# Modulation held in row blocks of two tiles, c kept on chip, and a reordered end of the convolution, in a decoder layer with a convolution mixer

## The chip, the cores and the metric

The kernel runs on 1 core of one Trainium2 chip. The metric is the device time of one execution in microseconds (us), median of several runs.

## The reference

One decoder layer with a convolution mixer: 256 tokens, model width 2048, all in float32. Cut to what matters:

```python
cond = silu(c)                                    # c: [1, 2048]
sh1, sc1, g1, sh2, sc2, g2 = split(cond @ mod_w + mod_b, 6)     # mod_w: [2048, 6*2048]
h = rms_norm(x, norm1_g) * (1 + sc1) + sh1
u = h @ conv_w_in + conv_b_in                     # [2048, 4096]
a, gt = split(u, 2)
u = depthwise_causal_conv(a * sigmoid(gt), conv_dw_w, width=31) + conv_dw_b
u = silu(layer_norm(u, conv_ln_g, conv_ln_b))
x = x + (1 + g1) * (u @ conv_w_out + conv_b_out)  # [2048, 2048]
h = rms_norm(x, norm2_g) * (1 + sc2) + sh2
x = x + (1 + g2) * (square(relu(h @ mlp_w1)) @ mlp_w2)          # 2048 -> 8192 -> 2048
```

## The kernel before, in words

Activations are held transposed: the 2048 features are 16 tiles of 128 partitions, the 256 tokens lie along the free axis. Every weight is loaded once from HBM as a 1 MB block (128 partitions, 16 feature tiles, 128 outputs) into a ring called `raw` of 5 buffers; all loads go through SyncE's queue in one list, `order`, topped up by `top_up` whenever `take` hands a buffer out. The load order is thus fixed, and a load waits until the buffer five loads earlier is free.

**Splitting.** To get float32 accuracy from the fast matmul format, a weight is split into `hi` (ScalarE, L174) and `lo` (VectorE or GpSimd, L175), six half-block buffers each; activations are split in the same way (`split_act`, L182 and L183). `mm` (L190, L191) then issues, for each of the 16 feature tiles, a 512-wide matmul (hi weight times hi and lo activation, side by side) and a 256-wide one (lo weight times hi activation, added to the second half). The two halves of the result are added afterwards by `evac` (ScalarE L391, VectorE L392).

**Jobs.** A job is two output tiles, 32 steps of `mm`. There are 16 `in` jobs (a tile of a and its gate), 8 `out` jobs, and four quarters of 8 `up` and 8 `down` jobs. The first 7 `in` jobs are computed beforehand, with the feature tile as the outer loop, into "held" PSUM tiles: their weights come as `first` blocks (one for each feature tile, 896 KB, ring of 3) and `first_mm` (L442 for unsplit float32 tiles named in `NATIVE`, else L448 to L450) adds one feature tile to all 14 held outputs.

**Modulation.** The product with mod_w is done in two ways. By rows: `mod_chunk` (L208) multiplies a 1 MB chunk (4 chunks make 512 outputs over all 2048 inputs) with the conditioning vector as weights; `mod_finish` (L255) turns the row into columns and adds biases. By columns: `mod_col` (L266) has VectorE multiply a transposed 1 MB block with a broadcast copy of silu(c) and sum along the row. The start takes tiles 0 to 7 of sh1 and sc1 by rows, in two blocks of four tiles (`BY_ROW`; 8 chunks before the first `first_mm`, then 8 more between its steps), and tiles 8 to 15 by columns. g1, sc2, half of sh2 (40 chunks) and the other half of sh2 (8 columns, after loading c again) come between the `in` and `out` jobs, so many for each job as `LATE_IN` and `LATE_OUT` say; g2 comes in the first quarter of the MLP.

**Convolution.** Nine tiles are convolved on VectorE (31 taps, L542), seven on TensorE (`PE_TILES`): `flatten` and `widen` send the tile through DRAM to lay out shifted copies, `pe_conv` (L655) multiplies with diagonal blocks. `CONV_AT` says after which job each is done; tile 15 uses on-chip copies (`copy_wide`, L633 and L635). Then `stats`, `fold_stats` and `add_stats` (L588, L598, L604, L605) sum the tiles and their squares, the layer-norm factor follows on ScalarE and VectorE (L760 to L764), and each pair of tiles is normalised, put through SiLU and split for the `out` jobs (L769 to L774). The eight chunks that `LATE_IN` gives to the last `in` job lie between these steps.

**Out and norm 2.** After each `out` job two tiles are biased, gated with g1, added to x, squared and scaled by sc2 (L789 to L810). The first two `up` jobs work on activations not yet normalised; the shift sh2 enters them through `shift_row` (L223), late in the first of them.

The order of instructions on each engine is chosen by the framework's scheduler from the program order, from `urgent` (priority) and from `tc.issue_after` (not ahead of the named instruction).

## Time and profile before

| | |
|---|---|
| Time, median of 3 runs | 1167.33 us (1166.96 to 1167.51) |
| Profiled execution: its own time | 1166.77 us |
| Profiled execution: span from first to last instruction | 1164.9 us |
| Mean granted TensorE clock | 0.987 of full |
| TensorE matmul busy | 1125.4 us (97% of the span) |
| VectorE, ScalarE, GpSimd busy | 731.3, 555.9, 167.0 us |
| Read from HBM | 295.70 MB, 256 GB/s over the span |

The time of a run is the span and 1.9 us around it. A matmul's "busy" counts its whole passage through a pipelined array, so the distance between the starts of two matmuls, not their durations, tells the cost of one. In the profile PE is TensorE, PEld its weight load, DVE VectorE, ACT ScalarE, POOL GpSimd, SP SyncE; L208 is line 208 of the kernel. The stages, by the trace: held jobs and their modulation until 143.6 us, `in` jobs until 304.9, end of the convolution and its norm until 338.2, `out` jobs until 435.1, then the MLP.

### The profile page before, as it was taken

The page shows a single profiled execution, that of the slowest core. Times are in us where ns is not written, and L with a number is a line of the kernel's source. Part 1 is how long each engine was busy: PE and PEld are TensorE (multiplying, and loading weights), DVE is VectorE, ACT ScalarE, POOL GpSimd, SP SyncE. Part 2 cuts the span into 40 slices and gives each one's busy share as a digit, 9 for nine tenths or more (in the row PEclk, how much of TensorE's full clock was granted, in tenths as well). Part 3 has the DMA queues.
Part 4 walks back from the last instruction along what each step waited for, and adds up shares of the span by engine and source line. Part 5 has one row for each costly group of instructions (what it writes and reads, how often), then busy time and mean ns, then how long its engine had stood idle before and what let it go on. Part 6 is the DMA issues. An engine that isn't in the chain of part 4 may idle for free.

```text
span 1164.9 us, 17233 instructions
## 1 busy us (share of the span) xinstructions
PE 1125.4 (97%) x6992; PEld 933.1 (80%) x6992; DVE 731.3 (63%) x1018; ACT 555.9 (48%) x730; POOL 167.0 (14%) x106
## 2 busy tenths in 40 slices
PE   5799999999989999999999999999999999999998
PEld 3579865766648888888888888888888888888886
DVE  1359689995336986888776554655555655555653
ACT  3352533333366668655444555434564444655431
POOL 0000185656352236000000000000000000000000
PEclk9799999999989999999999999999999999999999
DMA  9998989999887874788787555555554555555630
GB/s 388 397 420 361 406 294 385 343 380 321 307 322 263 314 256 181 291 318 300 283 303 275 185 195 169 210 181 185 190 201 171 194 184 187 201 187 181 205 131 28
DMA packets 46160, 299.81 MB, mean 257 GB/s; under 512 B 5120, under 2 KB 9344, under 8 KB 12416
## 3 DMA queue, kind: packets, MB, share of 16 engines
q1 hardware_dynamic: 45792, 297.99, 69.6%
q8 instruction: 55, 0.90, 0.3%
q10 hardware_dynamic: 288, 0.71, 0.2%
q14 instruction: 25, 0.20, 0.0%
HBM read 295.70 MB, written 2.98 MB: 256 GB/s over the span
## 4 chain that ended last, share of the span: by engine, by line
PE 84%; DVE 8%; DMA 4%; ACT 2%; issue 1%; POOL 0%; SPq 0%; ACTq 0%; DVEq 0%
PE mm L190 50%; PE mm L191 25%; PE row L208 3%; DVE raw L266 3%; DVE acc L542 2%; DMA wide<-flat 1%; DVE lo L430 1%; DMA first<-w_first 1%; PE small L289 1%; PE mm L655 1%; DMA raw<-w_in 1%; DMA flat<-u 1%; PE mm L450 1%; PE mm L448 1%; DMA x<-x 1%
## 5 line engine op out<-in xcount | busy, mean ns | idle before, releaser
L174 ACT ACTIVATE hi<-raw 128x1024 fp32r<-128x1024 f32 x324 | 341.4, 1058 | 425.1 <-PE mm L190 387.3
L190 PE MATMUL mm<-hl,hi 128*128 128x512 f32 x1504 | 530.7, 396 | 4.1 <-DVE u L668 2.2
L175 DVE TENSOR_TENSOR lo<-raw,hi 128x1024 fp32r<-128x1024 f32 x272 | 333.0, 1228 | 227.5 <-ACT hi L174 225.3
L191 PE MATMUL mm<-hl,lo 128*128 128x256 f32 x1504 | 423.5, 282 | 0.0
L190 PE MATMUL mm<-u,hi 128*128 128x512 f32 x1088 | 384.7, 397 | 0.0
L190 PEld LDWEIGHTS mm<-hl,hi 128*128 128x128 f32 x1504 | 282.8, 188 | 83.3 <-issue 14.1
L191 PE MATMUL mm<-u,lo 128*128 128x256 f32 x1088 | 306.5, 282 | 0.0
L191 PEld LDWEIGHTS mm<-hl,lo 128*128 128x128 f32 x1504 | 285.3, 190 | 8.5 <-issue 7.5
L190 PEld LDWEIGHTS mm<-u,hi 128*128 128x128 f32 x1088 | 204.2, 188 | 50.5 <-issue 0.2
L191 PEld LDWEIGHTS mm<-u,lo 128*128 128x128 f32 x1088 | 205.1, 189 | 0.0
L175 POOL TENSOR_TENSOR lo<-raw,hi 128x1024 fp32r<-128x1024 f32 x52 | 124.4, 2406 | 77.9 <-ACT hi L174 77.1
L542 DVE SCALAR_TENSOR_TENSOR acc<-u,v,acc 128x256 f32<-128x256 f32 x252 | 102.8, 487 | 0.9
L266 DVE SCALAR_TENSOR_TENSOR raw<-raw 128x2048 f32<-128x2048 f32 x24 | 57.5, 2396 | 33.4 <-DMA raw<-mod_c 33.3
L208 PE MATMUL row<-raw,cz 128*32 128x512 f32 x448 | 60.9, 610 | 10.7 <-DMA raw<-mod_r 10.7
L391 ACT ACTIVATE two<-mm 128x512 f32<-128x512 f32 (+1 forms) x74 | 42.5, 574 | 34.7 <-PE mm L191 34.2
L392 DVE TENSOR_TENSOR two<-mm,two 128x512 f32<-128x512 f32 (+1 forms) x65 | 43.9, 676 | 14.8 <-ACT two L391 13.6
L430 DVE TENSOR_TENSOR lo<-first,hi 128x896 fp32r<-128x896 f32 x24 | 25.4, 1088 | 38.3 <-ACT hi L429 38.3
L183 DVE TENSOR_TENSOR u<-two,u 128x512 fp32r<-128x512 f32 x40 | 31.4, 786 | 22.5 <-ACT u L182 22.4
L448 PE MATMUL mm<-hl,hi 128*128 128x256 f32 x96 | 29.4, 312 | 8.7 <-ACT hl L182 8.7
L266 DVE SCALAR_TENSOR_TENSOR raw<-raw,cond 128x2048 f32<-128x2048 f32 x16 | 36.3, 2286 | 1.8 <-ACT cond L282 1.8
L208 PEld LDWEIGHTS row<-raw,cz 128*32 128x32 f32 x448 | 10.4, 109 | 30.9 <-DMA raw<-mod_r 16.5
L429 ACT ACTIVATE hi<-first 128x896 fp32r<-128x896 f32 x24 | 21.7, 940 | 17.9 <-DMA first<-w_first 16.5
(144 smaller groups left out, 722.6 us busy)
## 6 DMA issues: line engine op xcount, KB each, us to landing
raw<-w SPq DMA_DIRECT2D x128, 1024.0 KB, 4.8
raw<-mod_r SPq DMA_DIRECT2D x56, 1024.0 KB, 8.3
raw<-mod_c SPq DMA_DIRECT2D x40, 1024.0 KB, 7.4
raw<-w_in SPq DMA_DIRECT2D x18, 1024.0 KB, 8.0
raw<-w_out SPq DMA_DIRECT2D x16, 1024.0 KB, 7.1
first<-w_first SPq DMA_DIRECT2D x16, 896.0 KB, 10.3
wide<-flat SPq DMA_DIRECT2D x24, 142.0 KB, 9.3
x<-x SPq DMA_DIRECT2D x2, 1024.0 KB, 7.6
```

The source lines that it names most:

```text
L174: nc.scalar.activation(hi, w[:, ks, :], AF.Copy)
L175: end = engine.tensor_tensor(lo, w[:, ks, :], hi.bitcast(F32), op=ALU.subtract)
L183: nc.vector.tensor_tensor(dst[:, :, T : 2 * T], src, dst[:, :, 0:T].bitcast(F32), op=ALU.subtract)
L190: nc.tensor.matmul(p[:, c, :], hi[:, k % HALF, :], m, start=(k == 0), stop=(k == KT - 1))
L191: state["mm_end"] = nc.tensor.matmul(p[:, c, T : 2 * T], lo[:, k % HALF, :], m[:, 0:T], start=False, stop=(k == KT - 1), skip_group_check= ...
L208: state["row_end"] = nc.tensor.matmul(row_ps[0][32 * k : 32 * k + 32, :], cz[:, 4 * kg + k, 3 - b : 35 - b], w[:, 4 * k : 4 * k + 4, :], s ...
L266: nc.vector.scalar_tensor_tensor(w, w, 1.0, cb, op0=ALU.mult, op1=ALU.mult, accum_out=acc)
L391: nc.scalar.activation(t1, p[:, cs, T : 2 * T], AF.Copy)
L392: nc.vector.tensor_tensor(t2, p[:, cs, 0:T], t1, op=ALU.add)
L430: nc.vector.tensor_tensor(lo, w[:, js, :], hi.bitcast(F32), op=ALU.subtract)
L448: nc.tensor.matmul(p, hi[:, j, :], m[:, 0:T], start=begin, stop=False, skip_group_check=True)
L542: nc.vector.scalar_tensor_tensor(out, s, w, acc, op0=ALU.mult, op1=ALU.add)
```

## The change

- **Start.** Tiles 0 to 7 of sh1 and sc1 come in four blocks of two tiles, 4 chunks each (`pair_chunk`, a new chunk layout of 8 feature tiles by 256 outputs). After each block its two tiles are modulated and multiplied; those steps lie between the chunks of the next block (`STEPS`). c is loaded ahead of the fourth block and its silu is kept (`cond`). The `first` ring has 5 buffers, and the unsplit tiles are 9, 11, 13, 15 instead of 8, 10, 12, 14.
- **Later modulation.** All 16 tiles of sh2 come by columns: 32 chunks and 16 columns instead of 40 chunks, c and 8 columns.
- **End of the convolution.** Tiles 12 and 14 are also copied on chip. The last `in` job computes its gate first. Sums of the first eight tiles move into the job before; the rest is put in a written order, with one chunk ahead of the last sums, six after them and one after the norm. The inverse root has one operation less on its path.
- **Merged products.** `mm(..., merged=True)` adds three 256-wide products into one 256-wide result, in the last `in` job, the `out` jobs and the last `down` job; their `evac` goes. The `out` jobs fold b_out into gb = (1 + g1) * b_out.
- **Memory.** Some temporaries move to other pools, and the padding ahead of the MLP's buffers is 40 instead of 64 columns.

```diff
-BY_ROW = (0, 1)
-NATIVE = (8, 10, 12, 14)
-GROUPS += [[4 * w + b for b in range(n)] for w, n in ((G1, 4), (SC2, 4), (SH2, 2))]
+PAIRS = 4
+NATIVE = (9, 11, 13, 15)
+GROUPS = [[4 * w + b for b in range(4)] for w in (G1, SC2)]
-FIRST = 3
+FIRST = 5
+COPIED = (12, 14, 15)
+PADDING = 40
-LATE_IN = [0] * 7 + [4, 3, 4, 3, 4, 3, 4, 3, 8]
-LATE_OUT = [2, 2, 2, 2, 2, 1, 1, 1]
+STEPS = (3, 3, 3, 2)
+LATE_IN = [0] * 7 + [3] * 8 + [8]
+LATE_OUT = [3, 3, 2, 2, 2, 2, 1, 1]
...
+    def mm(p, c, key, acts_of, ks=range(KT), merged=False):
...
+            if merged:
+                out_p, begin, end = p[:, c, 0:T], k == 0, k == KT - 1
+                w = hi[:, k % HALF, :]
+                nc.tensor.matmul(out_p, w, m[:, 0:T], start=begin, stop=False)
+                nc.tensor.matmul(out_p, w, m[:, T : 2 * T], start=False, stop=False)
+                state["mm_end"] = nc.tensor.matmul(out_p, lo[:, k % HALF, :], m[:, 0:T], start=False, stop=end)
+                continue
...
+    def pair_chunk(w, g, kg):
+        wt = take(("grp", w, g, kg))
+        begin, end = w == 0 and kg == 0, w == 1 and kg == 1
...
+        for k in range(8):
+            q = k % 4
+            state["row_end"] = nc.tensor.matmul(
+                row_ps[0][32 * q : 32 * q + 32, 0 : 2 * P], cz[:, 8 * kg + k, 3 - w : 35 - w], wt[:, 2 * k : 2 * k + 2, :],
+                start=begin and k < 4, stop=end and k >= 4,
+            )
...
-        nc.scalar.activation(guess, ms, AF.Abs_reciprocal_sqrt)
+        nc.scalar.activation(guess, src, AF.Abs_reciprocal_sqrt, scale=scale, bias=eps)
         nc.scalar.activation(q, guess, AF.Square)
+        nc.scalar.activation(guess, guess, AF.Copy, scale=-0.5)
-        nc.vector.tensor_tensor(ms, ms, q, op=ALU.mult)
-        nc.vector.tensor_scalar(ms, ms, -0.5, 1.5, op0=ALU.mult, op1=ALU.add)
-        nc.vector.tensor_tensor(r, ms, guess, op=ALU.mult)
+        nc.vector.scalar_tensor_tensor(ms, ms, EPS, q, op0=ALU.add, op1=ALU.mult)
+        nc.vector.scalar_tensor_tensor(r, ms, 3.0, guess, op0=ALU.subtract, op1=ALU.mult)
...
+    for g in range(PAIRS):
+        n = scaled(g, r1)
+        for at, key in enumerate(first[g]):
+            with tc.issue_after(state["step_end"].ins) if g else ExitStack():
+                mods([key])
+            with tc.issue_after(state["row_end"].ins):
+                step(STEPS[at])
+        with tc.issue_after(state["step_end"].ins) if g else ExitStack():
+            mod_finish()
...
+        with tc.issue_after(state["fold_end"].ins):
+            for _ in steps:
+                pass
+        modulate(g, n, SH1, SC1, two())
+        for k in range(2 * g, 2 * g + 2):
+            split_first(k)
+        steps = chain(first_mm(2 * g), first_mm(2 * g + 1))
+        if g == PAIRS - 2:
+            mods([("c", 0)])
     for k in BY_COL:
...
-        split_first(k - 1)
-        steps = chain(steps, first_mm(k - 1, h_last if k > 8 else None))
+        split_first(k)
+        h_last = h[:, c, :]
+        steps = chain(steps, first_mm(k, h_last))
...
+            for c in range(2) if i < KT - 1 else (1, 0):
...
-                sg = gate(i, evac(p, out=p[:, :, 0:T]))
+                gate(i, evac(p, out=p[:, :, 0:T]) if i < KT - 1 else p[:, :, 0:T])
+                if i in COPIED:
+                    copy_wide(i)
...
+            if n == KT - 2:
+                with tc.issue_after(state["mm_end"].ins):
+                    for b in range(2):
+                        stats(b)
...
             sq15 = two()
-            with urgent():
-                pe_conv(15, sq15[:, 1, :])
+            with tc.issue_after(state["conv_end"].ins):
                 stats(2)
...
                 st = fold_stats()
...
+                add_stats(st, [(cv(k), sq[:, k - 12, :]) for k in range(12, 14)], False)
+            with urgent(), tc.issue_after(state["sum_end"].ins):
+                pe_conv(15, sq15[:, 1, :])
...
+            with tc.issue_after(state["conv_end"].ins):
+                add_stats(st, [(cv(14), sq[:, 2, :])], False)
+            with tc.issue_after(state["sum_end"].ins):
+                mods(rows[:1])
+            with urgent(), tc.issue_after(state["row_end"].ins):
+                add_stats(st, [(cv(15), sq15[:, 1, :])], True)
...
-            mods(after[job])
+            with tc.issue_after(state["sum_end"].ins):
+                mods(rows[1:-1])
...
+            with tc.issue_after(state["row_end"].ins):
+                mods(rows[-1:])
...
-                nc.scalar.activation(
-                    t1[:, c, :], p[:, c, T : 2 * T], AF.Identity, bias=col("b_out", 2 * i + c)
-                )
-            nc.vector.tensor_tensor(t2, p[:, :, 0:T], t1, op=ALU.add)
+                nc.scalar.activation(t2[:, c, :], t2[:, c, :], AF.Identity, scale=mcol(G1, k), bias=gb[:, k : k + 1])
+            xp = pair_of(xs, i)
+            nc.vector.tensor_tensor(xp, t2, xp, op=ALU.add)
...
-                t2 = evac(p, cs)
+                t2 = evac(p, cs) if n < len(jobs) - 1 else p[:, cs, 0:T]
```

More of the change, by code (lines that the diff above doesn't have):

```diff
@@ L65, in conv_block @@
 @with_exitstack
-def conv_block(ctx: ExitStack, tc: tile.TileContext, x, vec, dwq, c_row, mod_r, mod_c, w_first, w_in, w_out, w1, w2, out):
+def conv_block(ctx: ExitStack, tc: tile.TileContext, x, vec, dwq, c_row, mod_q, mod_r, mod_c, w_first, w_in, w_out, w1, w2, out):
     nc = tc.nc
@@ L137, in home @@
     def home(key):
-        return key[0] if key[0] in ("first", "x") else "cond" if key == ("c", 0) else "raw"
+        return key[0] if key[0] in ("first", "x") else "cond" if key[0] == "c" else "raw"
     def top_up():
@@ L197, in conv_block @@
     pending = []
+    def pair_chunk(w, g, kg):
+        wt = take(("grp", w, g, kg))
+        begin, end = w == 0 and kg == 0, w == 1 and kg == 1
+        if begin:
+            mod_finish()
+            row_ps.append(ps.tile([P, 512], F32, name="row", bufs=1))
+        for k in range(8):
[4 more added lines that the diff above has]
+            )
+        if end:
+            r = tmp.tile([P, 512], F32, name="rowsb", bufs=1)
+            with urgent():
+                nc.scalar.activation(r[:, 0 : 2 * P], row_ps.pop()[:, 0 : 2 * P], AF.Copy)
+            pending.append(([v * KT + 2 * g for v in (SH1, SC1)], 2, r))
     def mod_chunk(nb, kg):
@@ L635, in copy_wide, with make_diag @@
                     nc.scalar.activation(dst, src, AF.Copy)
-    def pe_conv(ct, sq=None):
-        if sq is not None:
-            copy_wide(ct)
-        wide = wides.pop(ct)
-        diag = cp.tile([P, 32, 32], F32, name="diag", bufs=2)
+    diags = {}
+    def make_diag(ct):
+        diags[ct] = cp.tile([P, 32, 32], F32, name="diag", bufs=2)
         at = PE_TILES.index(ct)
@@ L649, in pe_conv @@
             )
-        p = ps.tile([P, 2, 2 * T], F32, name="mm", bufs=2)[:, 0, 0:T]
+    def pe_conv(ct, sq=None):
+        wide = wides.pop(ct)
+        diag = diags.pop(ct)
+        p = ps.tile([P, 2, 2 * T], F32, name="mm", bufs=2)[:, 0, 0:T] if sq is None else ps_two()[:, 0, :]
         if ct >= UNSHIFTED:
@@ L695, in conv_block @@
             continue
+        for ct in CONV_AT.get(n, ()) + ((15,) if n == KT - 1 else ()):
+            if ct in PE_TILES:
+                make_diag(ct)
         if n < len(jobs) - 1:
@@ L721, in conv_block @@
             for c in range(2):
-                mm(p, c, job + (c,), u2 if kind == "down" else hl)
+                mm(p, c, job + (c,), u2 if kind == "down" else hl, merged=kind == "out" or n == len(jobs) - 1)
         mod_finish()
```

158 lines of the change are left out of this document (64 added, 94 removed).

## The prediction

> **What bounds the kernel now.** I read the page first, then busy time by stage (windows cut at the stages' borders), then PE's waits, then the timeline at each border.
>
> ```profile
> PE 1125.4 (97%) x6992; PEld 933.1 (80%) x6992; DVE 731.3 (63%) x1018; ACT 555.9 (48%) x730; POOL 167.0 (14%) x106
> ```
>
> ```profile
> 0.00:142.00 142.00, 117.88 (x780) 97.19 (x781) 75.72 (x106) 53.10 (x76) 2.93 (x12) 0.93 0.97 398
> 145.50:305.00 159.50, 157.17 (x1160) 107.50 (x1160) 128.64 (x315) 50.58 (x65) 102.35 (x47) 1.00 0.94 338
> 305.00:338.10 33.10, 27.55 (x260) 12.60 (x258) 10.35 (x29) 18.17 (x36) 14.40 (x11) 0.97 0.83 329
> 338.10:435.10 97.00, 96.95 (x545) 81.90 (x546) 74.14 (x85) 63.59 (x102) 24.27 (x18) 0.97 0.78 288
> ```
>
> The columns are stretch, length, busy time of PE, PEld, DVE, ACT, POOL, granted clock, DMA share, GB/s. The held-job stage loads at 398 GB/s with the DMA engines 97% busy, and PE is also nearly full once it starts; the `in` stage is PE; the end of the convolution (33.1 us) has PE idle for 5.5 us; the `out` stage is PE. From 447 us on PE runs without a break and the change touches nothing there but the last job. So it can win in four places: the start, PE work taken out, the 33 us tail, and the very end.
>
> ```profile
> PE row L208 <- DMA raw<-mod_r: 3.4, 1, 3.4
> PE mm L190 <- DVE hl L183: 1.9, 1, 1.9
> ```
>
> These are two of the three waits of PE after 290 us (the third is 0.3 us): both lie in the tail, so whatever else is slow there is work queued in the wrong order, not an empty queue.
>
> **Start.** Before, eight row chunks precede the first `first_mm`.
>
> ```profile
> 27.16 1.06 PE L208 MATMUL row<-raw,cz 128*32 128x512 f32 x8 [1.42 <-DMA raw<-mod_r]
> 29.60 1.93 PE L208 MATMUL row<-raw,cz 128*32 128x512 f32 x8 [1.37 <-DMA raw<-mod_r]
> ...
> 41.28 0.80 PE L448 MATMUL mm<-hl,hi 128*128 128x256 f32 x2 [7.17 <-ACT hl L182]
> ...
> 143.36 0.28 PE L450 MATMUL small<-hl,lo 128*128 128x256 f32 x1
> ...
> 145.55 0.50 PE L190 MATMUL mm<-hl,hi 128*128 128x512 f32 x1 [1.92 <-DVE u L668]
> ```
>
> Chunks land 2.44 us apart. Four instead of eight bring the first `first_mm` forward by 4 x 2.44 = 9.8 us, from 41.3 to 31.5. That gain isn't kept, because PE then has more to do before the stage's end: four more chunks fall behind it (1.07 us each, next fence: 4.3) and two more foldings with their wait for the modulated tiles, which I put at 1 us of folding each. The stretch from 41.28 to the last held matmul at 143.36 + 0.12 is 102.2 us, so PE alone would end at 31.5 + 102.2 + 4.3 + 2 = 140.0. DMA sets another floor.
>
> ```profile
> raw<-mod_r SPq DMA_DIRECT2D x56, 1024.0 KB, 8.3
> ...
> first<-w_first SPq DMA_DIRECT2D x16, 896.0 KB, 10.3
> ```
>
> Two MB of x, 16 chunks, c and 16 columns are 35 blocks of 1024 KB, with 16 of 896 KB 51.4 MB; with the 0.7 MB of small vectors 52.1 MB. At 398 GB/s that is 131 us. Behind it comes tile 15, now unsplit, at 0.216 us for each of 28 passes:
>
> ```profile
> 117.30 0.28 PE L448 MATMUL mm<-hl,hi 128*128 128x256 f32 x1
> ...
> 117.66 0.28 PE L448 MATMUL mm<-hl,hi 128*128 128x256 f32 x1
> ...
> 120.54 3.62 PE L442 MATMUL mm<-two,first 128*128 128x256 f32 x16
> ...
> 124.00 1.89 PE L442 MATMUL acc<-two,first 128*128 128x256 f32 x8
> ```
>
> 16 passes in 3.46 us, so 6.1 us: DMA ends at 137. PE's 140.0 is the later; the gates behind it stay (2 us). **-3.5 us**, from 0 (the blocks' gaps eat it) to -6.5 (DMA's floor).
>
> The Trainium skill (DMA: Bandwidth & Descriptors, Where 436 GB/s comes from) says that a core's loads from HBM are bound at about 358 GB/s. By that the start's 52.1 MB would need 146 us and end 12 us later than I put it. The trace disagrees: 398 GB/s over 142 us.
>
> **`in` jobs.** Four chunks fewer (28 to 24).
>
> ```profile
> 145.50:305.00 159.50, 29.98 (x224) 4.82 (x224) 1.00 0.94 338
> 305.00:338.10 33.10, 10.56 (x72) 2.28 (x72) 0.97 0.83 329
> 338.10:435.10 97.00, 2.99 (x24) 0.57 (x24) 0.97 0.78 288
> ```
>
> L208 alone, eight instructions a chunk: 28, 9 and 3 chunks in the three stages, 1.07 us each in the first. PE is the bound there, so 4 x 1.07 = -4.3. The sums of eight tiles come in from the tail (+1.8, below). Merging the last job costs PE 0.36 us a step (three starts, 117.30 to 117.66) against 0.35 (343.35 to 343.70, below): +0.2 for 32 steps. Copying tiles 12 and 14 on chip costs for each what tile 15 costs now:
>
> ```profile
> 308.40 2.52 DVE L633 COPY wide<-u 32x284 f32<-32x284 f32 x8
> ```
>
> ```profile
> 309.27 3.58 ACT L635 ACTIVATE wide<-u 32x284 f32<-32x284 f32 x8
> ```
>
> That is 3.6 us of ACT and 2.5 of DVE; DVE has 31 us spare in this stage, ACT more, so nothing, and if that cover is gone at most the 5 us of DVE. It also takes eight `widen` loads and two `flatten` stores out of SP's queue. **-2.3 us.**
>
> **Tail.** From the last `in` matmul to the first `out` matmul it takes 33.3 us.
>
> ```profile
> 289.61 3.80 PE L655 MATMUL mm<-wide,diag 128*32 128x256 f32 x62
> ...
> 304.63 0.28 PE L191 MATMUL mm<-hl,lo 128*128 128x256 f32 x1
> ...
> 305.27 0.41 PE L588 MATMUL small<-sq,ones 128*32 128x256 f32 x2
> ...
> 306.16 3.62 PE L208 MATMUL row<-raw,cz 128*32 128x512 f32 x32
> ...
> 329.30 0.59 PE L605 MATMUL mm<-two,ones 128*128 128x256 f32 x2
> ...
> 338.15 0.76 PE L190 MATMUL mm<-hl,hi 128*128 128x512 f32 x1 [1.94 <-DVE hl L183]
> ```
>
> ```profile
> 330.62 0.43 DVE L762 TENSOR_SCALAR small<-mm 128x256 f32<-128x256 f32 x1 [12.09 <-ACT mu L761]
> ```
>
> Before, tile 14 waits for its copies from DRAM, the chunks run first (four at 306.16), and every chunk that PE takes ahead of the last sums delays the norm. After, with t0 = 304.9: tile 14 is convolved at once (0.4 for the shift, 3.5 for 64 passes: the 62 at 289.61 span 3.80, the last one's passage of 0.4 included): t0 + 3.9. The sums of four tiles, 0.9 (305.27 to 306.16), ScalarE's copy of them 0.6 (an operation on 256 columns of PSUM takes 0.43 at 330.62, and two hand-offs), fold 0.9 and four sums 1.7 (six passes of the same width as the shift's 0.4): t0 + 8.0. Tile 15, whose copies ended long before, 3.9: t0 + 11.9. Its evacuation 0.6, covered by a sum and the one chunk left here, then the last two sums: t0 + 14.8. I add 1 us because ScalarE must now put copies (3.6), evacuations and squares between these steps: t0 + 15.8. The norm comes after it: from the last sum (329.30 and its passes, 329.7) to 338.15 it is 8.4 us before; one VectorE operation like that of 0.43 goes ahead of the guess and one behind it, with their hand-offs 1.0: 7.4. Six chunks (6.4 us) run under it on PE. Total 23.2 instead of 33.3: **-10.1 us**, from -12 to -6 (the sums slip behind ScalarE by a whole tile's copies and squares, 4 us more).
>
> **`out` jobs.** Three chunks were there; one is left (1.1 instead of 3.2), and merging adds 8 x 32 x 0.007 = 1.8 by the rows quoted. Before, PE began this stage at half clock:
>
> ```profile
> 342.12 0.63 PE L190 MATMUL mm<-hl,hi 128*128 128x512 f32 x1
> ...
> 342.76 0.62 PE L190 MATMUL mm<-hl,hi 128*128 128x512 f32 x1
> ...
> 343.35 0.40 PE L190 MATMUL mm<-hl,hi 128*128 128x512 f32 x1
> ...
> 343.70 0.40 PE L190 MATMUL mm<-hl,hi 128*128 128x512 f32 x1
> ```
>
> A step is 0.64 us until 343.3 and 0.35 after it: 8 steps, 2.3 us lost. With PE busy under the norm this should go, but what is late next is ScalarE, which makes the eight normalised pairs:
>
> ```profile
> L182 ACT ACTIVATE hl<-acc 128x512 fp32r<-128x512 f32 x16 | 9.2, 583 | 0.1
> L773 ACT ACTIVATE acc<-two,v 128x256 f32<-128x256 f32 x16 | 8.7, 561 | 1.1 <-DVE two L770 0.7 <-DVE hl L183 0.3
> ```
>
> Two of 0.56 and one of 0.58 make 1.7 us a pair against PE's 1.44 (four steps of 0.36): I keep 1.0 of the 2.3. Against that stands loading. The tail's first chunk is now used at t0 + 13.9, and until then five buffers are full and no load starts; in the tail before, DMA moved 329 GB/s. The eight additional columns replace three chunks and c. At 2.62 us a block (1.05 MB at 398 GB/s) the last chunk lands at t0 + 23.7; behind it stand two weights for `out` 1, x (2 blocks), three columns, and the first weight of `out` 2 is ready at t0 + 47.1, when PE would want it at t0 + 46.2; that of `out` 3 comes 1.5 us late; then PE is again the slower. At the in-stage's slower rate it would be more: I take 4.0 us, between 0 and 10. VectorE gets 18.9 us more columns:
>
> ```profile
> 338.10:435.10 97.00, 18.89 (x16) 0.97 0.78 288
> ```
>
> (L266 alone, eight columns.) It was busy for 74 of 97 and loses some 7 in the simpler update of x, so 86: it fits, off PE's path. -2.1 + 1.8 - 1.0 + 4.0 = **+2.7 us**.
>
> **End.** The last evacuation goes.
>
> ```profile
> 1159.31 0.39 ACT two L391
> ...
> 1161.06 0.48 DVE x L849
> ```
>
> Two updates of 0.48 directly after PE instead of four steps until 1161.5: **-1.3 us**.
>
> Sum: -3.5 - 2.3 - 10.1 + 2.7 - 1.3 = -14.5. The profiled execution took 1166.77 (span 1164.9 and 1.9 around it), so 1152.3; the median of the runs is 0.56 higher: **1152.8 us**.
>
> **Rivals.** *The tail keeps its length*: the scheduler puts chunks or tile 15's copies ahead of what the sums need, as now; only the shorter norm (1.0) remains of 10.1: 1161.9. For it: 18 of 33 us of the tail are ScalarE's, and it gets more. Against: tile 14 no longer waits for DRAM, and the order of the sums is written out.
>
> *The start runs cold*: with four blocks PE waits at each border for folding, biases, modulation and split (41.28 shows 7.2 us for two pairs). If each of three borders costs a spell at half clock of 2.3 us, 6.9 us: 1159.7. The Trainium skill (TensorE: Matmul & The Clock Gate, Why this matters for your kernels) asks for no PE gap over about 3 us between bursts. The trace agrees in the tail: waits of 3.4 and 1.9 us, then 0.64 us a step; the 1.9 us wait at 145.55 by itself had no such step behind it.
>
> *The `out` stage starves* (slower): from the last chunk to the first weight of `up` 0, 32 blocks or 33.6 MB must land. PE allows about 90 us for it, and I have counted 4 more. If DMA only does there what it did in this stage before, 288 GB/s, it takes 117 us, 23 us more than counted: 1175.6. Break-even is at 14.5 us more, 33.6 MB in 108 us, 310 GB/s. Against: 288 was at a share of 0.78, with demand and not the engines as limit.
>
> *Nothing is gained*, each win covered by a new wait: 1167.
>
> **How the numbers follow.** Forecast 0.55; tail keeps its length 0.16; cold start 0.15; `out` starves 0.10; nothing gained 0.04 (half of it within the bound). A measurement of this kernel tells 0.2% (2.3 us) from no change. The forecast's own bounds go from 1143 (start -6.5, tail -12, `out` with no load wait) to 1161 (start 0, tail -6, a little more load wait); the range takes in the cold start and most of the lasting tail and leaves out the slow cases: 1143 to 1164. Faster 0.87, same 0.03, slower 0.10.
>
> **What would show it.** Right: the first L448 near 31 us, the first L190 near 142; last `in` matmul to first `out` matmul about 23 us with L655 of tile 14 first; 256 instead of 448 instructions of row chunks at `mod_chunk`'s line; one or two waits on `raw<-w_out` early in the `out` jobs. Wrong: steps of 0.64 us or waits on row chunks between 45 and 90 us; PE waiting on ScalarE in the tail; PE or VectorE waiting on loads through all `out` jobs.

## The result

The changed kernel takes 1154.03 us (median of 4 runs, 1153.37 to 1154.77) against 1167.42 before (4 runs, 1166.96 to 1167.66): ratio 0.9886, 95% interval 0.9869 to 0.9903. The profiled execution has a span of 1151.7 us (own time 1154.09). 1152.8 was predicted, with 1143 to 1164 as range. The total came out right, but by luck: two of its terms did not, and their errors, one in each direction, cancel.

PE's row of the page, and busy time by stage of the changed kernel (stretch, length, busy time of PE, PEld, DVE, ACT, POOL, granted clock, DMA share, GB/s):

```profile
PE 1113.2 (97%) x7368; PEld 953.2 (83%) x7368; DVE 752.8 (65%) x1033; ACT 560.8 (49%) x737; POOL 176.3 (15%) x106
```

```profile
144.00:306.50 162.50, 157.17 (x1171) 109.38 (x1172) 135.93 (x332) 58.15 (x81) 102.34 (x63) 0.99 0.83 297
306.50:329.80 23.30, 20.58 (x225) 9.95 (x224) 8.52 (x20) 14.42 (x31) 7.76 (x7) 1.00 0.42 167
329.80:431.70 101.90, 98.97 (x789) 96.92 (x786) 87.74 (x90) 63.05 (x95) 36.65 (x20) 0.97 0.96 368
431.70:1148.00 716.30, 716.16 (x4270) 634.32 (x4269) 442.79 (x480) 366.64 (x447) 21.98 (x8) 1.00 0.58 209
```

The MLP's row of the kernel before, which the prediction didn't show:

```profile
435.10:1159.30 724.20, 724.17 (x4240) 632.50 (x4238) 439.69 (x478) 366.31 (x447) 19.53 (x8) 1.00 0.58 206
```

The shares of the whole hardly moved; the lengths of the stages did. The `in` stage and the `out` stage are longer than before, the tail is 10 us shorter, and the MLP, where "the change touches nothing", is 8 us shorter with PE busy throughout in both kernels.

For all kernels the stages are cut alike, in us of the one profiled execution of each: until the first `in` matmul; to the last `in` matmul (in); to the first `out` matmul (tail); to the first `up` matmul (out); to the end of PE's last matmul's pass (MLP); the rest of the span (end).

| | until in | in | tail | out | MLP | end | span |
|---|---|---|---|---|---|---|---|
| before | 145.6 | 159.1 | 33.5 | 96.9 | 724.0 | 5.8 | 1164.9 |
| changed | 144.1 | 162.3 | 23.5 | 101.9 | 715.9 | 4.0 | 1151.7 |
| difference | -1.5 | +3.2 | -10.0 | +5.0 | -8.1 | -1.8 | -13.2 |
| predicted | -3.5 | -2.3 | -10.1 | +2.7 | 0 | -1.3 | -14.5 |
| after_pad64 | 144.4 | 163.3 | 24.3 | 101.3 | 729.3 | 4.1 | 1166.7 |
| before_pad40 | 145.9 | 159.1 | 33.5 | 97.3 | 722.0 | 5.7 | 1163.5 |
| before_addr | 146.7 | 161.4 | 33.5 | 96.3 | 716.9 | 5.9 | 1160.7 |
| after_shift32 | 143.0 | 163.3 | 24.4 | 102.3 | 716.3 | 4.1 | 1153.4 |
| tail_order | 142.6 | 161.3 | 27.7 | 94.8 | 718.6 | 4.1 | 1149.1 |
| copied15 | 143.2 | 163.7 | 30.3 | 101.5 | 716.6 | 3.9 | 1159.2 |
| copy01 | 144.6 | 165.0 | 26.3 | 102.1 | 720.3 | 4.1 | 1162.4 |
| evac01 | 144.2 | 162.3 | 24.0 | 101.8 | 720.5 | 4.0 | 1156.8 |
| fix_in | 142.1 | 154.7 | 24.4 | 102.3 | 717.3 | 4.0 | 1144.8 |
| combo1 | 141.6 | 153.5 | 27.7 | 96.3 | 715.9 | 4.1 | 1139.0 |
| combo2 | 143.7 | 154.9 | 27.7 | 95.3 | 715.9 | 4.0 | 1141.6 |
| combo3 | 142.7 | 155.1 | 24.5 | 95.8 | 715.9 | 4.1 | 1138.1 |

How far a row can be trusted shows in stages that an edit left alone. The `in` stage of before_addr, with the same instructions as before, is 2.3 us longer than that of before (161.4 and 159.1); the MLPs of copy01, evac01, tail_order and fix_in are 1 to 5 us longer than the changed kernel's because PE waits in their first `down` quarter, while the other steps are spaced as there.

Two of PE's waits in the `in`, tail and `out` stages of the changed kernel (what waited for what: total us, times, longest; at `issue` the profile shows nothing that PE waited for); the first is new, the second was 3.4 us at once before:

```profile
PE mm L677 <- issue: 3.4, 1, 3.4
...
PE row L239 <- DMA raw<-mod_r: 2.5, 3, 2.0
```

And its timeline at the borders (start, us, engine, line, operation, count, idle time before it and what ended that):

```profile
30.37 0.80 PE L482 MATMUL mm<-hl,hi 128*128 128x256 f32 x2
...
144.06 0.50 PE L203 MATMUL mm<-hl,hi 128*128 128x512 f32 x1 [3.34 <-DVE u L692]
144.52 0.40 PE L203 MATMUL mm<-hl,hi 128*128 128x512 f32 x1
144.87 0.40 PE L203 MATMUL mm<-hl,hi 128*128 128x512 f32 x1
...
306.95 3.66 PE L677 MATMUL mm<-wide,diag 128*32 128x256 f32 x64
...
321.47 0.59 PE L624 MATMUL mm<-two,ones 128*128 128x256 f32 x2
...
328.84 1.06 PE L239 MATMUL row<-raw,cz 128*32 128x512 f32 x8 [1.98 <-DMA raw<-mod_r]
329.83 0.48 PE L199 MATMUL mm<-hl,hi 128*128 128x256 f32 x1
330.55 0.41 PE L199 MATMUL mm<-hl,hi 128*128 128x256 f32 x1
331.19 0.41 PE L199 MATMUL mm<-hl,hi 128*128 128x256 f32 x1
...
359.04 0.39 PE L199 MATMUL mm<-hl,hi 128*128 128x256 f32 x1 [2.17 <-ACT hi L180]
360.30 0.39 PE L201 MATMUL mm<-hl,lo 128*128 128x256 f32 x1 [0.76 <-DVE lo L181]
...
361.67 0.41 PE L199 MATMUL mm<-hl,hi 128*128 128x256 f32 x1
362.31 0.41 PE L199 MATMUL mm<-hl,hi 128*128 128x256 f32 x1
```

The tail goes step by step as it was worked out: tile 14 at once, the last sums done 15.3 us after the last `in` matmul's pass (predicted 15.8), the first `out` matmul 23.2 us after it (predicted 23.2). But `out` begins at half clock, a step of 0.64 us again, and at its third job PE waits 2.9 us for weights, with half clock behind that wait too.

### The profile page after: what moved, and what is told of

It is laid out like the page before. It is cut to its first block, busy times and chain, and to the rows that moved or that the text cites. A ratio compares the mean times of both kernels' runs of the same rounds, so it can differ in the third digit from the quotient of the medians.

```text
span 1151.7 us, 17985 instructions
## 1 busy us (share of the span) xinstructions
PE 1113.2 (97%) x7368; PEld 953.2 (83%) x7368; DVE 752.8 (65%) x1033; ACT 560.8 (49%) x737; POOL 176.3 (15%) x106
## 4 chain that ended last, share of the span: by engine, by line
PE 84%; DMA 8%; DVE 5%; ACT 2%; issue 1%; SPq 0%; POOL 0%; DVEq 0%; ACTq 0%; POOLq 0%
PE mm L203 43%; PE mm L204 23%; PE mm L201 4%; PE mm L199 3%; PE mm L200 3%; DVE raw L297 3%; DMA first<-w_first 3%; DMA wide<-flat 2%; PE row L239 2%; PE mm L677 2%; DMA raw<-mod_q 2%; DMA x<-x 1%; DVE lo L464 1%; DMA flat<-u 1%; PE row L220 1%
## 5 line engine op out<-in xcount | busy, mean ns | idle before, releaser
L203 PE MATMUL mm<-hl,hi 128*128 128x512 f32 x1216 | 426.5, 394 | 3.3 <-DVE u L692 3.3
L203 PE MATMUL mm<-u,hi 128*128 128x512 f32 x1056 | 366.8, 390 | 0.0
L204 PE MATMUL mm<-u,lo 128*128 128x256 f32 x1056 | 297.7, 282 | 0.0
L203 PEld LDWEIGHTS mm<-hl,hi 128*128 128x128 f32 x1216 | 227.6, 187 | 70.3 <-issue 16.8
L203 PEld LDWEIGHTS mm<-u,hi 128*128 128x128 f32 x1056 | 198.2, 188 | 41.7 <-issue 0.2
L204 PEld LDWEIGHTS mm<-u,lo 128*128 128x128 f32 x1056 | 199.6, 189 | 0.1
L297 DVE SCALAR_TENSOR_TENSOR raw<-raw,cond 128x2048 f32<-128x2048 f32 x48 | 112.4, 2350 | 8.3 <-DMA raw<-mod_c 6.4
L199 PE MATMUL mm<-hl,hi 128*128 128x256 f32 x288 | 82.7, 289 | 2.2 <-ACT hi L180 2.2
L200 PE MATMUL mm<-hl,hi 128*128 128x256 f32 x288 | 82.8, 288 | 0.0
L199 PEld LDWEIGHTS mm<-hl,hi 128*128 128x128 f32 x288 | 56.3, 197 | 4.5 <-ACT hi L180 2.4
L200 PEld LDWEIGHTS mm<-hl,hi 128*128 128x128 f32 x288 | 56.7, 197 | 0.4 <-issue 0.4
L425 ACT ACTIVATE two<-mm 128x512 f32<-128x512 f32 x71 | 41.3, 581 | 13.2 <-PE mm L204 13.2
L426 DVE TENSOR_TENSOR two<-mm,two 128x512 f32<-128x512 f32 x63 | 43.1, 684 | 4.0 <-ACT two L425 4.0
```

Of the source, the lines that this page charges most:

```text
L199: nc.tensor.matmul(out_p, w, m[:, 0:T], start=begin, stop=False)
L200: nc.tensor.matmul(out_p, w, m[:, T : 2 * T], start=False, stop=False)
L203: nc.tensor.matmul(p[:, c, :], hi[:, k % HALF, :], m, start=(k == 0), stop=(k == KT - 1))
L204: state["mm_end"] = nc.tensor.matmul(p[:, c, T : 2 * T], lo[:, k % HALF, :], m[:, 0:T], start=False, stop=(k == KT - 1), skip_group_check= ...
L297: nc.vector.scalar_tensor_tensor(w, w, 1.0, cb, op0=ALU.mult, op1=ALU.mult, accum_out=acc)
L425: nc.scalar.activation(t1, p[:, cs, T : 2 * T], AF.Copy)
```

## The experiments

Every ratio below is to runs of the kernel before on the same chip. Four questions were open: what made the MLP faster, what the tail's parts are worth, what lengthened the `in` stage, and whether the answers make a better kernel.

### Where the buffers lie

**after_pad64**

```diff
-PADDING = 40
+PADDING = 64
```

> The changed kernel with PADDING 64 instead of 40: the u2 buffers lie 96 bytes lower, at the addresses that they had before the change, and nothing else moves. In the kernel before, the steps that read u2 were spaced 0.3534 us on average, in the changed kernel 0.3467; 1088 steps read u2. Theory 'address': the place of u2 in SBUF alone sets this, so the steps return to about 0.353 and the run takes 1088 x 0.0067 = 7 us more, about 1161. Rival 'traffic': the other moves or the missing work did it, u2's place does nothing: the steps stay at 0.347 and the time at 1154.

Measured: 1169.03 us (10 runs, 1163.22 to 1171.06, a wide scatter), ratio 1.0011, interval 0.9994 to 1.0027. The whole gain of the change is gone, about twice what "address" expected to lose. The first matmul of three consecutive groups of 256 steps (hl, u2, hl), before the change, in the changed kernel and in after_pad64:

```profile
621.51 0.40 PE L190 MATMUL mm<-hl,hi 128*128 128x512 f32 x1
...
710.27 0.39 PE L190 MATMUL mm<-u,hi 128*128 128x512 f32 x1
...
800.71 0.40 PE L190 MATMUL mm<-hl,hi 128*128 128x512 f32 x1
```

```profile
615.07 0.39 PE L203 MATMUL mm<-hl,hi 128*128 128x512 f32 x1
...
703.82 0.40 PE L203 MATMUL mm<-u,hi 128*128 128x512 f32 x1
...
792.58 0.39 PE L203 MATMUL mm<-hl,hi 128*128 128x512 f32 x1
```

```profile
619.99 0.39 PE L203 MATMUL mm<-hl,hi 128*128 128x512 f32 x1
...
710.43 0.39 PE L203 MATMUL mm<-u,hi 128*128 128x512 f32 x1
...
800.87 0.39 PE L203 MATMUL mm<-hl,hi 128*128 128x512 f32 x1
```

Divide each distance by 256. Before: 88.76 us for hl (0.3467 a step), 90.44 for u2 (0.3533). Changed: 88.75 and 88.76. after_pad64: 90.44 and 90.44. So the steps on u2 return to their old spacing, as "address" says, and those on hl, whose buffers didn't move, slow down as well. PE waits for nothing in any of these stretches and its granted clock is 1.00: what differs is the spacing of matmuls that follow each other.

**before_pad40**

```diff
-            pad.tile([P, 64], F32, name="pad")
+            pad.tile([P, 40], F32, name="pad")
```

> The kernel before with the padding of 40 columns instead of 64, so that only its u2 buffers move, by 96 bytes. Theory 'address': the steps on u2 go from 0.3534 to 0.347 and the run takes 7 us less, about 1160. Rival 'traffic': no change, 1167.

Measured: 1164.99 us (10 runs, 1163.83 to 1174.41), ratio 0.999, interval 0.9972 to 1.0008. The MLP is 2 us shorter, not 7: in its first quarter all steps are spaced 0.353, later those on hl 0.3467 and those on u2 0.349. Neither theory has a third spacing, nor one that changes while the buffers stay: hl's lie where they lay in the first quarter. u2's place alone isn't enough.

**before_addr**

```diff
+    shim = const.tile([P, 8], F32, name="shim")
+    nc.gpsimd.memset(shim, 0.0)
...
-            pad.tile([P, 64], F32, name="pad")
+            pad.tile([P, 40], F32, name="pad")
```

> The kernel before with the padding of 40 columns and 32 more bytes in the first pool, so that raw, hi, lo, hl and u2 all lie as far past a multiple of 128 bytes as in the changed kernel (32, 32, 32, 32 and 64 bytes); one small memset is added and no other instruction changes. Theory 'addresses': the spacing of the MLP's steps is set by where these buffers lie; all of them come to 0.347 us, the MLP takes 7 us less than before: about 1160. Rival 'traffic': what sets it is the other work of the kernel before, and the steps on u2 stay at 0.3534: 1166.

Measured: 1160.97 us (1159.59 to 1162.55), ratio 0.995, interval 0.9934 to 0.9967.

```profile
622.27 0.39 PE L192 MATMUL mm<-hl,hi 128*128 128x512 f32 x1
...
711.02 0.40 PE L192 MATMUL mm<-u,hi 128*128 128x512 f32 x1
...
799.77 0.39 PE L192 MATMUL mm<-hl,hi 128*128 128x512 f32 x1
```

88.75 us for both. The kernel before, with nothing of the change but where its buffers lie, has the changed kernel's MLP (716.9 us against 724.0). That is the changed kernel's 8.1 us, but for 1 us; this lies in the first `up` job, where sh2 enters and one pair of steps is 4.8 us apart instead of 5.8. What the intended parts of the change brought is then the distance from here to the changed kernel, some 7 us (1160.97 and 1154.03).

**after_shift32**: the same `shim` in the changed kernel.

> The changed kernel with the same 32 more bytes in the first pool: raw, hi, lo and hl lie at 64 past a multiple of 128 bytes instead of 32, u2 stays. Theory 'addresses': the weights and hl move against u2, so some of the MLP's steps leave 0.3467 us; at 0.3534 for one kind 7 us more (1161), for both 15 us more (1169). Rival 'u2 alone': only the place of u2 counts and nothing changes: 1154.

Measured: 1153.34 us (1149.56 to 1164.25, four runs that scatter widely), ratio 0.99, interval 0.9847 to 0.9953. In the profiled execution all steps stay at 0.3467 but those of the merged last job, which go from 0.350 to 0.360 us. Moving weights and hl by 32 bytes against u2 does next to nothing here. So placement moves the spacing, but no rule of offsets comes out: by the offsets in the expectations, hl at 32 bytes past a multiple of 64 is fast in the changed kernel, u2 at the same offset is slow in after_pad64, and a slow u2 leaves hl fast in one kernel and slow in another.

### The parts of the tail

**tail_order**: the end of the convolution in the order of before, with the on-chip copies kept.

```diff
-            if n == KT - 2:
-                with tc.issue_after(state["mm_end"].ins):
-                    for b in range(2):
-                        stats(b)
...
+            for b in range(2):
+                stats(b)
             sq15 = two()
-            with tc.issue_after(state["conv_end"].ins):
+            with urgent():
+                pe_conv(15, sq15[:, 1, :])
                 stats(2)
...
-            with tc.issue_after(state["sum_end"].ins):
-                mods(rows[1:-1])
+            mods(rows)
```

> The changed kernel with the order of the end of the convolution as before: tile 15 is convolved with high priority, the sums of the first eight tiles are in the tail again, and the eight row chunks are free to go ahead of the last sums. The on-chip copies of tiles 12 and 14 stay, as does the shorter inverse root. Theory 'order': the written order brings most of the tail's 9.8 us; chunks ahead of the sums cost up to 7 x 1.07 and the eight tiles' sums 1.8, so the tail grows from 23.4 to about 31 and the run takes 7 to 9 us more, about 1162. Rival 'copies': the tail was long because tile 14 waited for its copies from DRAM; the order is worth 1 to 3 us, about 1156.

Measured: 1152.27 us (1151.04 to 1155.2), ratio 0.9885, interval 0.9867 to 0.9902: level with the changed kernel. Both theories expected it slower.

```profile
313.67 4.49 PE L239 MATMUL row<-raw,cz 128*32 128x512 f32 x35
...
322.08 0.59 PE L624 MATMUL mm<-two,ones 128*128 128x256 f32 x2
```

```profile
303.90:331.60 27.70, 22.76 (x251) 12.58 (x249) 9.05 (x27) 16.84 (x34) 8.95 (x8) 0.94 0.66 271
331.60:426.40 94.80, 94.64 (x770) 93.98 (x771) 90.17 (x83) 61.51 (x94) 36.90 (x19) 0.98 0.95 361
```

Chunks stand ahead of the last sums again, and the tail is 4.2 us longer (27.7 instead of 23.5). The `out` stage, in turn, is 7.1 us shorter: the first five chunks give their buffers back some 5 us earlier, DMA moves 271 GB/s in the tail instead of 167, and the wait at the third `out` job is gone with the half clock behind it (2.9 and some 1.7 us); most of the rest are the last chunk and its folding, which are done before `out` begins instead of in it. What the written order wins in the tail it gives back one stage later.

**copied15**

```diff
-COPIED = (12, 14, 15)
+COPIED = (15,)
```

> The changed kernel with tiles 12 and 14 copied through DRAM again; only tile 15 is copied on chip. The written order of the tail, which starts with tile 14, stays. Theory 'copies': tile 14's copies land after the last in matmul, and now everything in the tail stands behind them: the tail grows from 23.5 by 5 to 10 us, about 1161. Rival 'ready': tile 14's gate is done a job earlier and its copies land under the last in job: 1153 to 1155.

Measured: 1158.94 us (1154.28 to 1161.3), ratio 0.9919, interval 0.9889 to 0.9949. In the profiled execution, the slowest of the four, the tail is 30.3 us, 6.8 longer:

```profile
312.94 5.04 PE L677 MATMUL mm<-wide,diag 128*32 128x256 f32 x64 [5.26 <-DMA wide<-flat]
```

A wait of 5.26 us for tile 14's copies, and half clock for part of its passes (5.04 us instead of 3.66). Of the tail's 10 us the on-chip copies bring 6.8 there; in the faster runs it may be less, as by the median the kernel loses 4.9. tail_order's 5.8 us (33.5 to 27.7, which has the copies but not the order) says much the same from the other side.

### The `in` stage

Between 162 and 188 us the traces part. ScalarE and PE of the changed kernel:

```profile
179.47 2.00 ACT L180 ACTIVATE hi<-raw 128x1024 fp32r<-128x1024 f32 x2 [4.42 <-DMA raw<-w_in]
181.38 0.45 ACT L690 ACTIVATE sg<-mm,v 128x256 f32<-128x256 f32 x1
181.73 0.46 ACT L683 ACTIVATE cv<-mm,v 128x256 f32<-128x256 f32 x1
```

```profile
175.25 3.66 PE L677 MATMUL mm<-wide,diag 128*32 128x256 f32 x64 [0.83 <-DMA wide<-flat]
182.30 5.35 PE L677 MATMUL mm<-wide,diag 128*32 128x256 f32 x64 [3.39 <-issue]
```

ScalarE of the kernel before in the same place:

```profile
178.25 0.47 ACT L666 ACTIVATE sg<-mm,v 128x256 f32<-128x256 f32 x1 [2.10 <-DVE mm L392]
183.69 2.00 ACT L174 ACTIVATE hi<-raw 128x1024 fp32r<-128x1024 f32 x2 [4.97 <-DMA raw<-w_in]
185.60 0.82 ACT L660 ACTIVATE cv<-mm,v 128x256 f32<-128x256 f32 x2
```

The wait for w_in is old, and so is the place of the convolutions' copies out of PSUM, where PE's sums lie (`cv`), behind the `hi` that waits. New is the gate of job 8 (`sg`): before, it ran ahead of that `hi`; in the changed kernel it stands behind it. In SyncE's queue the eight `wide` loads of tiles 0 and 1 (162.49 to 173.08) stand ahead of the two `w_in` loads, which are issued from 173.53 on.

**copy01**: the copies of tiles 0 and 1 on chip, so that nothing of theirs goes through SyncE's queue.

```diff
-            if i in PE_TILES:
-                flatten(i)
         for i in range(HELD):
             if i in PE_TILES:
-                widen(i)
+                copy_wide(i)
```

> The changed kernel, with the shifted copies of tiles 0 and 1 made on chip by ScalarE and VectorE instead of through DRAM. In the changed kernel PE has some 5.3 us of idle time between 172 and 181 us, and the convolution behind it runs at half clock (64 passes in 5.35 us instead of 3.66). Theory 'queue': the eight loads of those copies hold SyncE's queue from 162.5 to 173.1, the w_in loads behind them come late, and ScalarE waits 4.4 us for them with PE's next work behind it. Without the DRAM copies this goes: 4 to 7 us less, 1147 to 1150. Rival 'buffers': the w_in loads are late because the row chunks ahead of them free their buffers late, and the idle time stays: 1154 or, with 7 us more on ScalarE at the gates, up to 1158.

Measured: 1160.6 us, ratio 0.9954, interval 0.9939 to 0.997: some 7 us slower than the changed kernel, beyond even the rival's 1158 (the profiled execution, 1164.43, was the slowest of six). PE's waits from 100 to 300 us:

```profile
PE mm L677 <- DVE u L692: 7.1, 1, 7.1
PE mm L203 <- DVE u L692: 4.9, 1, 4.9
```

The w_in loads are issued from 166.06 on, without those eight in front, but the copies stand ahead of the held tiles' gates on VectorE and ScalarE and put the taps behind them back, and the second convolution still waits: now visibly for job 8's gate. That named what else might be held in the changed kernel.

**evac01**

```diff
-            if sq is None:
+            if sq is None and ct < SHIFT:
+                nc.vector.tensor_scalar(cv(ct), p, col("dwb", ct), None, op0=ALU.add)
+            elif sq is None:
                 nc.scalar.activation(cv(ct), p, AF.Identity, bias=col("dwb", ct))
```

> The changed kernel with one edit: the results of the convolutions of tiles 0 and 1 are copied out of PSUM by VectorE instead of ScalarE. Theory 'behind hi': between 172 and 182 us ScalarE's next instruction is a hi that waits 4.4 us for its w_in load; the copy of tile 0's result stands behind it, holds its PSUM buffer, and keeps tile 1's convolution from starting although its data are there. With the copy on VectorE tile 1 is convolved during the wait, its 64 passes run at full clock, and the in stage becomes 4 to 6 us shorter: about 1149. Rival 'loads': PE would wait for that w_in load anyway and only 0 to 2 us come back: 1152 to 1154.

Measured: 1151.97 us (1149.92 to 1158.77), ratio 0.9883, interval 0.9849 to 0.9917; the `in` stage is 162.3 us, as before the edit. (The profiled execution was the slowest of the four: it has a 2.7 us wait of PE in the MLP that the others may not have.) The theory fell in this form:

```profile
178.61 2.00 ACT L180 ACTIVATE hi<-raw 128x1024 fp32r<-128x1024 f32 x2 [3.82 <-DMA raw<-w_in]
180.52 0.46 ACT L692 ACTIVATE sg<-mm,v 128x256 f32<-128x256 f32 x1
```

```profile
181.79 6.14 PE L677 MATMUL mm<-wide,diag 128*32 128x256 f32 x64 [4.04 <-issue]
```

PE starts right after job 8's gate, whose `sg` is still behind `hi`. The convolutions and the jobs share two PSUM buffers; freeing one doesn't help while the gate holds the other.

**fix_in**: evac01, and the weights' splits may not go ahead of the held tiles' gate 1.

```diff
+        state["sg"] = nc.scalar.activation(sg, t2[:, 1, :], AF.Sigmoid, bias=col("b_in", KT + i))
...
+            if i == 1:
+                state["sg1"] = state["sg"].ins
...
-            splits(jobs[n + 1])
+            with tc.issue_after(state["sg1"]):
+                splits(jobs[n + 1])
```

> The changed kernel with two edits: VectorE copies the results of the convolutions of tiles 0 and 1 out of PSUM, and the split of a job's weights may not go ahead of gate 1 of the held tiles, which also puts job 8's gate ahead of the hi that waits for w_in. Theory 'two behind hi': moving the copy of tile 0 alone gave nothing in the in stage because job 8's PSUM buffer was held by its gate, which stands behind the same hi (at 178.6 to 180.5 us); with neither behind it tile 1 is convolved during the wait, at full clock: the first in matmul comes 2 us earlier and the in stage is 4 to 6 us shorter than 162.3, about 1147. Rival 'loads': the w_in load is what PE waits for, whatever is done meanwhile comes back as a wait: the in stage keeps at least 161 us, 1151 to 1154.

Measured: 1144.8 us (1143.44 to 1146.72), ratio 0.9805, interval 0.9789 to 0.9822. ScalarE and PE:

```profile
173.79 0.47 ACT L692 ACTIVATE sg<-mm,v 128x256 f32<-128x256 f32 x1 [0.77 <-DVE mm L426]
177.41 2.01 ACT L180 ACTIVATE hi<-raw 128x1024 fp32r<-128x1024 f32 x2 [3.15 <-DMA raw<-w_in]
```

```profile
173.20 7.09 PE L677 MATMUL mm<-wide,diag 128*32 128x256 f32 x128
```

`hi` waits for its load as before, but both convolutions run while it waits and splits, in one piece and at full clock. The `in` stage is 154.7 us, 7.6 shorter. PE's wait ahead of the first `in` matmul is 2.11 us instead of 3.34, here and in the three kernels below that keep this edit; that matmul comes 1.9 us earlier, the rest being held steps that end earlier, whose end varies by 2.3 us among kernels edited elsewhere. The rival ("loads") is out: w_in's lateness costs PE nothing once nothing stands behind it. That the gate moved ahead of `hi` at job 8 is the scheduler's doing after the new constraint, not an edit of its own. The constraint without evac01's edit wasn't run; the kernel before had its copies out of PSUM behind `hi` and no such wait, so it may be that the constraint alone does it.

### Better versions

**combo1** is fix_in with tail_order's tail; **combo2** is combo1 with

```diff
-LATE_UP = [0, 0, 1, 1, 1, 1, 2, 2]
-LATE_DOWN = [1] * 8
+LATE_UP = [0, 0, 0, 1, 1, 1, 1, 1]
+LATE_DOWN = [0, 0, 1, 2, 2, 2, 2, 2]
```

> The two edits of fix_in, and the end of the convolution in the looser order of tail_order. If the parts add: 2 us from the first gates, 4 to 6 from the in stage, and 3 from tail and out together (27.7 + 94.8 us instead of 23.5 + 101.9), so about 1144. Rival 'loads': what ends earlier meets later loads in the out stage and in the first quarter of the MLP, and half of it is lost: about 1149.

> combo1 with the sixteen columns of g2 spread later (0, 0, 0, 1, 1, 1, 1, 1 in the up jobs and 0, 0, 1, 2, 2, 2, 2, 2 in the down jobs of the first quarter). In some executions VectorE waits 2 to 3 us for a column around the first down job, PE's evacuation stands behind it, and with the half clock after it that quarter is 3 to 4 us longer. Theory 'columns': with fewer columns ahead of that point this wait goes: 0 to 4 us less than combo1, and less scatter between runs. Rival: the weights themselves are late there and nothing changes.

Measured: combo1 1141.19 us (1140.66 to 1141.99), ratio 0.9779, interval 0.9764 to 0.9793; combo2 1140.81 (1140.09 to 1143.6), ratio 0.978, interval 0.9765 to 0.9794. In combo1 the parts add (the sum was 1144, and it came 3 us better). The columns of combo2 change nothing, nor is the scatter any less: its rival.

**combo3**: fix_in and combo2's columns with the written tail, and two chunks right behind tile 14's convolution.

```diff
+            rows = list(after[job])
             with tc.issue_after(state["conv_end"].ins):
+                mods(rows[:2])
+            with tc.issue_after(state["row_end"].ins):
                 stats(2)
...
-            rows = list(after[job])
...
-                mods(rows[:1])
+                mods(rows[2:3])
...
-                mods(rows[1:-1])
+                mods(rows[3:-1])
```

> The two edits of fix_in and the columns of combo2, with the written order of the tail kept, but two of the eight row chunks put right behind tile 14's convolution instead of behind the last sums. Theory 'late buffers': the written order makes the out stage 7 us longer because five full buffers are held until 14 us into the tail and the weights of out 2 come late; two chunks 9 us earlier let two loads (5 us at 398 GB/s) start earlier, which covers the 3.0 us of waiting and the half clock behind it: the tail grows by 1 to 2 us to about 25.5, the out stage falls from 102 to about 96, and the run takes about 1140, level with combo1. Rival 'later': the lack of loads only moves to out 3 or beyond, the out stage stays above 100 us, and the run takes 1144 to 1147, no better than fix_in.

Measured: 1138.38 us (1136.56 to 1141.06), ratio 0.9752, interval 0.9733 to 0.9771, the fastest of all by its median; its interval overlaps those of combo1 and combo2.

```profile
297.80:322.30 24.50, 22.46 (x243) 11.44 (x241) 7.43 (x19) 14.21 (x31) 7.16 (x7) 1.00 0.61 235
322.30:418.10 95.80, 95.03 (x772) 94.19 (x772) 90.22 (x92) 62.94 (x96) 42.40 (x20) 0.98 0.96 378
```

Two buffers given back early bring DMA in the tail from fix_in's 178 to 235 GB/s. The tail is as long as fix_in's (24.5 against 24.4), the `out` stage 6.5 us shorter. "Late buffers" holds. Tail and `out` together take 120.3 us against combo1's 124.0, so by one profiled execution of each the written order is worth having once its chunks aren't all late.

## Why the prediction was right, and where not

**Start, -3.5: measured -1.5.** The first `first_mm` came at 30.37 (31.5 predicted) and the held steps end at about 140.6 (140.0). Some 1.3 of the 2.0 us missed are the gates' "2 us", which became 3.34: ScalarE splits two halves of weights between gate 0 and gate 1, and this now begins when PE ends instead of before. fix_in, which forbids that, took 1.2 us off this wait. The rest are the held steps, which end late although they begin early; a half-clock spell in them is shown below, with the rivals.

**`in`, -2.3: measured +3.2. This step failed.** It took PE as the bound and subtracted PE work. The saved chunks, the sums and the merging may well be worth -2.3 (with the order mended, fix_in is 4.4 us below before), but the step looked at nothing that is queued: it didn't ask which instructions stand behind the 4.97 us that ScalarE waits at 183.69 in the trace of before. There it was the convolutions' copies out of PSUM; in the changed kernel it is job 8's gate as well, both PSUM buffers are held, and PE loses 3.39 us of waiting and some 1.7 us of half clock behind it.

**Tail, -10.1: measured -10.0**, with its steps at their times. The cause given, tile 14's copies, has 5.8 of it by tail_order and 6.8 by copied15's profiled execution; that the other steps add up so closely is in part chance, as the same tail is 23.5 to 24.4 us long in the kernels that don't change it.

**`out`, +2.7: measured +5.0.** Waits for weights were sized at 4.0 and measured 2.9, at `out` 2 alone. The failed term is the half clock: 1.0 of 2.3 us should have gone; instead the first spell shrank only to some 1.7 us (half clock for 3.4) and a second of the same length followed the wait. Of the merging, a step of 0.36 us was right. With these sizes the sum is -2.1 + 1.8 - 0.6 + 1.7 + 2.9 = +3.7; some 1 us of the stage stays unexplained. The rival of a starving stage is out (368 GB/s, not 288); the full buffers held in the tail, for which the forecast had its 4.0 us, are what tail_order and combo3 took away.

**MLP, 0: measured -8.1. This step failed.** "The change touches nothing there" overlooked that the change moves the MLP's buffers: u2's by the padding of 40 instead of 64 columns, which had no line in the sum, the weights' and hl's by 32 bytes in the first pool. "PE runs without a break" was read as a fixed rate; it isn't, and before_addr shows 7.1 us of it from placement alone (2 us from the padding alone, by before_pad40).

**End, -1.3: measured -1.8.**

So +3.2 in the `in` stage where -2.3 stood, and -8.1 in the MLP where 0 stood, leave a sum only 1.3 us from the forecast. That is luck: without the MLP's 8.1 us, which nobody had meant to win, the run would have taken some 1162. A total that agrees is no proof of its terms.

Of the rivals, "the start runs cold" holds at one of the three borders, the last:

```profile
81.80 0.58 PE L483 MATMUL mm<-hl,hi 128*128 128x256 f32 x1 [2.79 <-DVE hl L189]
82.18 0.42 PE L484 MATMUL mm<-hl,lo 128*128 128x256 f32 x1
82.40 0.42 PE L482 MATMUL mm<-hl,hi 128*128 128x256 f32 x1
```

The passes are 0.21 us apart instead of 0.12, and the granted clock is 0.50 until 87.62: the held steps lose some 2.9 us (half of 81.80 to 87.62). At the other two borders PE waits 0.6 us or less and goes on at full clock. The kernel before has a like spell at 77.41, half as long, behind waits of 1.5 and 0.5 us; the prediction didn't see it.

The Trainium skill (TensorE: Matmul & The Clock Gate, Why this matters for your kernels) asks for no PE gap over about 3 us. The runs agree only in part: the 3.34 us wait at 144.06 has full steps right behind it (144.52 to 144.87), the waits of 2.79 us at 81.80 and 1.98 us at 328.84 half-clock steps.

## What to carry to other kernels

When work is taken from the engine that is the bound, list for every wait of the other engines what stands behind the waiting instruction and which buffers that holds: the two edits of fix_in, which remove no work, are worth 9 us, two thirds of what the whole change had gained (13.4). Of chunks that hold load buffers, put a few early even on the critical path: two of them cost nothing measurable and gave 6.5 us back one stage later. And compare the spacing of identical instructions in both traces before calling a stage untouched.

## What the hardware showed that was not expected

- Back-to-back matmuls of the same shapes, with no wait and a granted clock of 1.00, are spaced 0.3467, 0.349 or 0.3533 us a step, depending on where the buffers lie in SBUF (the on-chip memory that holds the tiles) by 32 to 96 bytes; over the MLP's 2,000 steps that is up to 13.4 us (715.9 against 729.3). The spacing is constant over hundreds of steps, while the other engines' work comes and goes, which speaks against traffic as its cause. But placement isn't all: in before_pad40 the steps on hl are 0.353 us apart in the first quarter and 0.3467 from 623.57 on, from the very step at which the operand changes from u2 back to hl, with the same buffers. What ran just before seems to count too; no run tested that. By which rule placement acts, and why hl slows down with u2 in after_pad64, stays open. The Trainium skill (SBUF — State Buffer, SBUF: two separate sides) says that PE's port never waits on another engine; nothing here speaks against that, but it leaves this difference without a cause.
- The length of a wait of PE isn't what half clock goes by alone: 3.34 us without it at 144.06, 1.98 us with it at 328.84, and in tail_order the same 3.34 us wait (at 142.63) with it. The granted clock on record shows a grid: in the changed kernel half clock begins at 80.79, 183.19, 329.96 and 360.68 us, which are 30, 43 and 9 times 3.413 us apart, and lasts 3.41 or 6.83 us. In the 3.41 us ahead of those four PE waits 2.0, 2.5, 2.0 and 2.5 us. The grid cuts the 3.34 us wait into 1.5 and 1.8, that of tail_order into 1.2 and 2.2. So it seems to be the idle share of one such window that counts. No sharp limit comes out: in tail_order one window with 1.4 us of waiting, amid row chunks, is followed by half clock, in before_pad40 one with 2.0 (ahead of 334.15) isn't. Row chunks use 32 of the 128 output columns; whether that matters wasn't tried.
